# Turning the gated features by VectorE blocks and SBUF transfers, and adding the last products by copy and accumulating transfer, in a fused encoder layer

## The chip, the cores and the metric

One Trainium2 chip, one of its cores. The metric is the device time of the whole layer in microseconds (us). The kernel before takes 1175.23 us, the median of three runs.

## What is computed

A hybrid encoder layer over 256 rows of 2048 features: a mixing part (neighbourhood attention beside a gated recurrence), a SwiGLU feed-forward part of width 5632, and a gated embedding at the end, each with RMS norms. The change lies in the feed-forward part:

```python
fn = rms_norm(h, g_ffn_pre[i])
ff = (jax.nn.silu(fn @ w_ffn_gate[i]) * (fn @ w_ffn_up[i])) @ w_ffn_down[i]
h = h + rms_norm(ff, g_ffn_post[i])
```

## The kernel before

Every product is in float32 precision from three products of rounded parts: a weight tile `w` (two blocks of 128 input features, 512 columns, 512 KB) is loaded by SP into a raw tile, ScalarE (ACT) rounds it to `wh` (L464), VectorE (DVE) takes `wl = w - wh` (L489), and TensorE (PE) multiplies the split activations `hi`, `lo` with `wh`, `wl`, `wh` (L528 to L530). Six slots hold `wh`/`wl` and four the raw tiles; tiles that other stages lend (`lent_w`, `lent_r`, `lent_t`) add to them.

The feed-forward part runs in three parts of 4, 4 and 3 gate groups. A gate group makes 512 gate and 512 up columns from eight pairs of input blocks. Five pairs are plain (kind `p`: two weight tiles, 24 matmuls); three are of kind `s`, Strassen's seven products: 21 matmuls, for which DVE forms two more weight tiles out of the two loaded (`lent_t`, L509 and L513). The seven products end in four banks `p1 p5 p6 p7` and four banks `c11 c21 c12 c22`. When a group's last `s` pair is done, `Seven.early` takes the p banks into the tiles `e` (printed `mid`) and `u_hi`, `u_lo`; when its last pair is done, `Gated.late` adds the four c banks to them on DVE (L1589). ACT takes silu of `e` (L1616), DVE multiplies by `u` (L1596).

The gated features then have the 256 rows on partitions, and w_ffn_down needs the features there. `transposed` (L315) turns them on PE, four 128x128 transposes for each two blocks, into a bank; `split` (L295 on ACT, L297 on DVE) makes `hi` and `lo` of it (`mid0h`, `mid0l`, and so on). After the gate groups of a part, two down groups (one in the last part, with two plain segments behind it) multiply with w_ffn_down. `DOWN` says in which order and kind they take the pairs of blocks; `mid_sums` makes the sums that `s` pairs need of the activations. `Down.late` adds the down products to `mg` in SBUF.

All instructions are written in the order that a planner (`Plan`) chooses at build time from a table of costs: each engine then runs its list in order, and an instruction whose inputs are late holds all that stand behind it on its engine. Weight loads stand in SP's list; each waits for a raw tile that DVE has released.

Of the kernel before, what the change touches and what calls it, by code (L numbers as in the profile page):

```python
# [16 lines left out]
P = 128  # L17
# [26 lines left out]
for _n, _w in (  # L44
# [10 lines left out]
T_BUFS = 2  # L55
W_MORE = 1
# [11 lines left out]
LATE_SUMS = 0.0  # L68
FIRST = "ppppspsp"
KINDS = "ppspspsp"  # L70
HALF = max(2 * KINDS.count("s") * 4 * P, 2 * 1024)
# [156 lines left out]

def dma(kb, take=None):
    return ("dma", kb / 340.0, None, take, None)  # L230
# [3 lines left out]
def layer(ctx: ExitStack, tc: tile.TileContext, a: dict, out: bass.AP):  # L234
# [6 lines left out]
        wr=R_BUFS, w=W_BUFS, ts=0, acc=ACC_BUFS, sm=SM_BUFS, ev=1, mid=2, bt=2, uv=1  # L241
# [36 lines left out]
    ones = const.tile([P, P], F32, name="ones")  # L278
    nc.gpsimd.memset(ones, 1.0)
# [63 lines left out]
    class Act:  # L343
# [10 lines left out]
        def blocks(self, hi, lo, base, n, first=0):  # L354
            for i in range(n):
                self.at[base + i] = (hi[:, first + i, :], lo[:, first + i, :])
# [18 lines left out]
    class Group:  # L375


        def __init__(self, w, n0, lhs, ks, kinds, post, after=None):
            self.after = after
            self.lhs, self.post, self.banks, self.i0 = lhs, post, {}, len(tiles)  # L380
            self.early = Event()
            self.units = list(zip(ks, kinds))
            self.early = Event()
            for (k, _), kind in self.units:
                i = len(tiles)
                tiles.extend((w[c], k, n0[c]) for c in range(2))
                by_dma.update({"d": (i, i + 1), "e": (i + 1,), "c": (i,)}.get(kind, ()))
                if kind == "s":
# [82 lines left out]
    def add_raw(i):  # L471
        yield added(512)
        nc.gpsimd.dma_start(los[i], raws[i], accum_op=ALU.add)
        landed = Event()
        landed.t = plan.now + LANDED
        yield landed
        done(ev_lo[i, 2])
        used(i)
# [40 lines left out]
    def products(i, kx, lhs, accs, ts, start, stop, at=0.0):  # L519
        for j in range(2):  # L520
            here = ev_lo[i, j + 1] if (i, j + 1) in ev_lo else ev_lo[i, 2]
            plan.main(6 * MM * len(ts) / NT, here, lhs.ev[kx + j], at=at)
            wh, wl = his[i], los[i]
            hi, lo = lhs.at[kx + j]
            for t in ts:
                sl = slice(t * P, (t + 1) * P)
                st, sp = start and j == 0, stop and j == 1
                nc.tensor.matmul(accs[t], hi[:, sl], wh[:, j, :], start=st, stop=False)  # L528
                nc.tensor.matmul(accs[t], hi[:, sl], wl[:, j, :], start=False, stop=False)  # L529
                nc.tensor.matmul(accs[t], lo[:, sl], wh[:, j, :], start=False, stop=sp)  # L530
            at_pe[0] = max(at_pe[0], i)
            if j:
                free_w(i)
            plan.run()
# [11 lines left out]
    def seven(i, kx, g, start, stop):  # L546

        for name, v, j, which in FORMS:
            n = i + v
            if isinstance(which, tuple):  # L550
                kk, t = which
                (hi, lo), ev = g.lhs.at[kx + kk], g.lhs.ev[kx + kk]
                hi, lo = hi[:, t * P : (t + 1) * P], lo[:, t * P : (t + 1) * P]
# [14 lines left out]
    def run_group(g, flip):  # L568
# [5 lines left out]
        strassens = [n for n, (_, kind) in enumerate(g.units) if kind == "s"]  # L574
        for n, ((_, kx), kind) in enumerate(g.units):
            if kind == "s":
                seven(i, kx, g, n == strassens[0], n == strassens[-1])
                i += 4
                if n == strassens[-1]:
                    plan.add(g.post.early(g), plan.clk["pe"] + plan.SEM)  # L580
                    plan.run()
                continue
# [7 lines left out]
        plan.add(g.post.late(g), plan.clk["pe"] + plan.SEM)  # L590
# [139 lines left out]
    def open_p1():  # L730
        t1["hs"], t1["rec_hi"] = big(0, "hs", F32), big(1, "rec_hi")
        p1 = p1_ctx.enter_context(tc.tile_pool(name="p1", bufs=1))
        t1["pool"] = p1
        xp = p1.tile([P, HB, S + 4], F32, name="xp")
# [23 lines left out]
        nc.gpsimd.memset(ssr, 0.0)  # L758
# [3 lines left out]
    ssr = const.tile([P, S], F32, name="ssr")  # L762
    ssa = const.tile([P, S], F32, name="ssa")
# [151 lines left out]
    def group_rstd(ss, name):  # L915
# [3 lines left out]
        nc.tensor.matmul(pb[:, 0, :], ones, ss, start=True, stop=True)  # L919
        rb = const.tile([P, S], F32, name=f"rb_{name}")  # L920
# [15 lines left out]
    def gate_pair(b0, b, e, ev):  # L936
# [9 lines left out]
        yield from add_squares(ssr, sq, False)  # L946
        done(ev)

    def yg_post(hf):
        def post(ch):  # L950
# [13 lines left out]
            rb = yield from group_rstd(ssr, "rec")  # L964
# [132 lines left out]
    def attend(g):  # L1097
        ph, pl, vh, vl, sq, attnT = (t1[n] for n in ("ph", "pl", "vh", "vl", "sqa", "attnT"))
        yield ev_v[g]
        for b in range(0, HB, 2):  # L1100
# [23 lines left out]
            yield from add_squares(ssa, sq, h == 0)  # L1124
# [3 lines left out]
        ra = yield from group_rstd(ssa, "attn")  # L1128
# [249 lines left out]
    def mid_sums(mid, ks):  # L1378
        rs = t2["pool"]
        a_ = rs.tile([P, 2, 2, 4, P], F32R, tag="ple0", name="sums_a")  # L1380
        b_ = rs.tile([P, 2, 4, P], F32R, tag="pT", name="sums_b")
        at_ = [(a_[:, n, 0, :, :], a_[:, n, 1, :, :]) for n in range(2)]
        at_.append((b_[:, 0, :, :], b_[:, 1, :, :]))
        for k, (hi, lo) in zip(ks, at_):
            mid.sums[k] = hi, lo
            yield mid.ev[k]
            yield mid.ev[k + 1]
            yield dve(2 * S, take="uv")
            v = at.tile([P, 2, NT, P], F32, tag="at0_hi", name="v")
            nc.vector.tensor_tensor(  # L1390
                out=v.rearrange("p k t m -> p k (t m)"), in0=f32(mid.pair_of(k, 0)),
                in1=f32(mid.pair_of(k, 1)), op=ALU.add,
            )
            yield from act_sums(mid, k, v)

# [18 lines left out]
    def transpose_h(b, hi, lo, nxt, gname):  # L1414
# [20 lines left out]
        yield from act_sums(nxt, b, v)  # L1435
# [20 lines left out]
    def act_sums(x, b, v):  # L1456

        s = at.tile([P, 4, P], F32, tag="at0_lo", name="s")
        for n, i0, i1, op in (
            (0, v[:, 0, 1, :], v[:, 1, 1, :], ALU.add),  # L1460
            (1, s[:, 0, :], v[:, 0, 0, :], ALU.subtract),
            (2, v[:, 0, 0, :], v[:, 0, 1, :], ALU.subtract),
            (3, v[:, 1, 0, :], s[:, 1, :], ALU.subtract),
        ):
            yield dve(P)
            nc.vector.tensor_tensor(out=s[:, n, :], in0=i0, in1=i1, op=op)
# [63 lines left out]
    class Mid(Act):  # L1530
        def __init__(self, name):
            super().__init__()
            self.name, self.halves = name, {}
# [8 lines left out]
        def pair_of(self, k, which):  # L1542
            i, j = divmod(k, 8)
            return self.halves[i][which][:, j : j + 2, :]
# [31 lines left out]
    class Gated(Seven):  # L1576


        def __init__(self, mid, kk0):
            self.mid, self.kk0 = mid, kk0  # L1580

        def late(self, g):
# [3 lines left out]
            gated = [Event() for _ in range(NT)]  # L1586
            for t, c, n, x in self.parts():
                yield dve(N)
                nc.vector.tensor_tensor(out=x, in0=bk[n], in1=x, op=ALU.add)  # L1589
                g.give(n)  # L1590
                if not c:
                    plan.add(self.silu(t, gated[t]), plan.now)
            for t in range(NT):
                yield gated[t]
# [4 lines left out]
                )  # L1599
            plan.free["uv"].append(plan.now)  # L1600
            for b in range(0, 4, 2):
                tr = yield from transposed(e, b, g.ring["c11"])
                if b == 2:
                    plan.free["mid"].append(plan.now)
                kk = self.kk0 + b
                i, j = divmod(kk, 8)
                hi, lo = self.mid.tiles(i)
                yield from split(
                    hi[:, j : j + 2, :], lo[:, j : j + 2, :], tr, 2 * S, give=g.ring["c11"]
                )  # L1610
                self.mid.pair(kk)

        def silu(self, t, ev):
# [7 lines left out]
    class Down(Seven):  # L1621
# [5 lines left out]
        def late(self, g):  # L1627
            yield g.early
            mg, c0 = t2["mg"], self.c0
            for t, c, n, x in self.parts():  # L1630
# [7 lines left out]
                g.give(n)  # L1638
            plan.free["mid"].append(plan.now)
# [4 lines left out]

    def after_ffn():
        return next_norm(ffn, hP, rstd_p, ev_rp, ("ple", "g_ple_post"))

    hF.ev_sums = {k: Event() for k, kind in zip(ORDER, KINDS) if kind == "s"}

    parts = ((0, 4), (4, 8), (8, 11))  # L1650
    for part, (f0, f1) in enumerate(parts):
        mid = Mid(f"mid{part}")
        for f in range(f0, f1):
            Group(("w_ffn_gate", "w_ffn_up"), (f * N, f * N), hF,
                  [(k, k) for k in ORDER], KINDS if f else FIRST, Gated(mid, (f - f0) * 4))
        last_lent[0] = len(tiles)
        last = part == len(parts) - 1
        units = [[(u[0], int(u[1:])) for u in us.split()] for us in DOWN[f1 - f0]]
        summed = []
        for us in units[:1] if last else units:  # L1660
            summed += [k for kind, k in us if kind == "s" and k not in summed]
        mid.ev_sums = {k: Event() for k in summed}
        for n in range(1 if last else 2):
# [3 lines left out]
                  after=(lambda mid=mid, ks=summed: plan.add(  # L1667
                      mid_sums(mid, ks), plan.clk["pe"], LATE_SUMS)) if n == 0 else None)
# [189 lines left out]
```

## Time and profile before

| | before |
|---|---|
| median of three runs | 1175.23 us (1174.59 to 1175.87) |
| profiled execution: own time, span | 1173.45 us, 1171.7 us |
| granted clock | 0.997 |
| busy PE, DVE, ACT | 1150.5, 961.3, 701.9 us |
| HBM read | 232.6 MB, 203 GB/s over the span |

The profile is of one execution. Busy times of an engine are sums over its instructions where they don't overlap; a matmul's recorded length is longer than the step to the next one, so PE looks busy also where small gaps lie, and the steps between starts are the better measure. The feed-forward part runs from about 405 to 1045 us of the span.

### The profile page before, as it was taken

The numbers are of one execution on the slowest core, as the hardware profiler recorded it, in microseconds if no ns is written. First come the engines' busy times: TensorE is split into PE (matmuls) and PEld (weight loads), VectorE is DVE, ScalarE is ACT, GpSimd is POOL, SyncE is SP. The second block draws the span as 40 slices with busy tenths as digits, with TensorE's granted clock in tenths as the row PEclk, the third lists the DMA queues.
The fourth block names the chain that finished last, engine by engine and source line by source line (L and its number), as shares of the span: only waits on it lengthen the run. The fifth ranks groups of instructions, "written<-read, shape, count | busy, mean of one in ns | idle before, by whom it ended". The sixth has DMA issues, their size and how long they took to land.

```text
span 1171.7 us, 14652 instructions
## 1 busy us (share of the span) xinstructions
PE 1150.5 (98%) x5259; PEld 951.6 (81%) x5259; DVE 961.3 (82%) x1267; ACT 701.9 (60%) x952; POOL 1.6 (0%) x13
## 2 busy tenths in 40 slices
PE   7999999999999999999999999999999999999996
PEld 5788888888888888888888888888888888887885
DVE  5677868778549898898989899889999989888663
ACT  6787777766548655563665556554536446466752
POOL 0000000000000000000000000000000000000000
PEclk9999999999999999999999999999999999999998
DMA  8855555545864865664775475575567456775751
GB/s 307 288 173 180 176 187 197 164 158 168 313 229 141 302 191 180 224 214 146 226 256 192 159 245 182 173 238 160 191 207 242 153 180 229 261 246 190 241 171 72
DMA packets 70344, 238.80 MB, mean 204 GB/s; under 512 B 7552, under 2 KB 13824, under 8 KB 68864
## 3 DMA queue, kind: packets, MB, share of 16 engines
q1 hardware_dynamic: 70128, 237.79, 60.9%
q8 instruction: 41, 0.67, 0.2%
q14 instruction: 31, 0.25, 0.1%
q10 hardware_dynamic: 144, 0.08, 0.0%
HBM read 232.60 MB, written 5.24 MB: 203 GB/s over the span
## 4 chain that ended last, share of the span: by engine, by line
PE 82%; DVE 6%; DMA 6%; ACT 3%; issue 1%; SPq 1%; DVEq 0%; ACTq 0%
PE c L528 12%; PE c L530 12%; PE c L529 12%; PE acc L530 9%; PE acc L528 9%; PE acc L529 9%; PE p L538 3%; PE p L539 3%; PE p L537 3%; DVE wl L489 3%; PE c L537 2%; PE c L538 2%; PE c L539 2%; PE tr L315 2%; DMA wr<-in_w_ffn_down 1%; DMA xs<-in_xT 1%
## 5 line engine op out<-in xcount | busy, mean ns | idle before, releaser
L489 DVE TENSOR_TENSOR wl<-wr,wh 128x1024 fp32r<-128x1024 f32 (+1 forms) x311 | 358.4, 1167 | 76.0 <-ACT wh L464 75.1
L464 ACT CAST wh<-wr 128x1024 fp32r<-128x1024 f32 (+1 forms) x311 | 307.8, 1008 | 138.8 <-PE acc L530 46.7
L528 PE MATMUL c<-wh,hT_mix_hi 128*128 128x512 f32 x400 | 157.4, 394 | 0.0
L530 PE MATMUL c<-wh,hT_mix_lo 128*128 128x512 f32 x400 | 155.9, 390 | 0.0
L529 PE MATMUL c<-wl,hT_mix_hi 128*128 128x512 f32 x400 | 155.8, 389 | 0.0
L464 ACT CAST wh<-lent_t 128x1024 fp32r<-128x1024 f32 x75 | 78.7, 1052 | 113.0 <-DVE lent_t L513 105.7
L528 PE MATMUL acc<-wh,hT_hi 128*128 128x512 f32 x320 | 127.9, 400 | 6.6 <-ACT wh L464 6.6
L529 PE MATMUL acc<-wl,hT_hi 128*128 128x512 f32 x320 | 125.6, 392 | 1.8 <-DVE wl L489 1.8
L530 PE MATMUL acc<-wh,hT_lo 128*128 128x512 f32 x320 | 125.5, 392 | 0.0
L489 DVE TENSOR_TENSOR wl<-lent_t,wh 128x1024 fp32r<-128x1024 f32 x75 | 89.6, 1218 | 1.3 <-ACT wh L464 1.1
L530 PEld LDWEIGHTS c<-wh,hT_mix_lo 128*128 128x128 f32 x400 | 75.1, 188 | 16.0 <-DVE hT_mix_lo L303 0.2
L529 PEld LDWEIGHTS c<-wl,hT_mix_hi 128*128 128x128 f32 x400 | 75.2, 188 | 15.0
L528 PEld LDWEIGHTS c<-wh,hT_mix_hi 128*128 128x128 f32 x400 | 75.1, 188 | 15.0
L489 DVE TENSOR_TENSOR wl<-lent_r,wh 128x1024 fp32r<-128x1024 f32 (+1 forms) x70 | 76.3, 1102 | 4.7 <-ACT wh L464 4.5
L464 ACT CAST wh<-lent_r 128x1024 fp32r<-128x1024 f32 (+1 forms) x70 | 65.1, 957 | 23.9 <-PE c L530 15.2
L528 PEld LDWEIGHTS acc<-wh,hT_hi 128*128 128x128 f32 x320 | 60.6, 189 | 18.1 <-ACT wh L464 6.6
L529 PEld LDWEIGHTS acc<-wl,hT_hi 128*128 128x128 f32 x320 | 60.4, 189 | 14.9 <-DVE wl L489 3.4
L530 PEld LDWEIGHTS acc<-wh,hT_lo 128*128 128x128 f32 x320 | 60.3, 189 | 12.7
L530 PE MATMUL acc<-wh,hT_ffn_lo 128*128 128x512 f32 x112 | 43.7, 390 | 0.9 <-DVE hT_ffn_lo L303 0.9
L528 PE MATMUL acc<-wh,hT_ffn_hi 128*128 128x512 f32 x112 | 44.0, 393 | 0.0
L529 PE MATMUL acc<-wl,hT_ffn_hi 128*128 128x512 f32 x112 | 43.6, 389 | 0.0
L1616 ACT ACTIVATE mid<-mid,rstd_f 128x512 f32<-128x512 f32 x22 | 14.7, 716 | 28.8 <-DVE mid L1589 28.8
(439 smaller groups left out, 2334.8 us busy)
## 6 DMA issues: line engine op xcount, KB each, us to landing
wr<-in_w_in SPq DMA_DIRECT2D x79, 512.0 KB, 4.4
wr<-in_w_ffn_down SPq DMA_DIRECT2D x68, 512.0 KB, 4.3
wr<-in_w_ffn_gate SPq DMA_DIRECT2D x60, 512.0 KB, 4.2
wr<-in_w_ffn_up SPq DMA_DIRECT2D x60, 512.0 KB, 4.7
wr<-in_w_out SPq DMA_DIRECT2D x32, 512.0 KB, 4.7
wr<-in_w_ple_gate SPq DMA_DIRECT2D x32, 512.0 KB, 4.3
lent_r<-in_w_ffn_gate SPq DMA_DIRECT2D x28, 512.0 KB, 4.2
lent_r<-in_w_ffn_up SPq DMA_DIRECT2D x28, 512.0 KB, 4.5
```

Of the source, the lines that this page charges most:

```text
L315: nc.tensor.transpose(tr[:, b, t * P : (t + 1) * P], src, ident)
L464: nc.scalar.copy(his[i][:, j, :], raws[i][:, j, :])
L489: nc.vector.tensor_tensor(out=los[i][:, j, :], in0=raws[i][:, j, :], in1=f32(his[i][:, j, :]), op=ALU.subtract,)
L528: nc.tensor.matmul(accs[t], hi[:, sl], wh[:, j, :], start=st, stop=False)
L529: nc.tensor.matmul(accs[t], hi[:, sl], wl[:, j, :], start=False, stop=False)
L530: nc.tensor.matmul(accs[t], lo[:, sl], wh[:, j, :], start=False, stop=sp)
L537: nc.tensor.matmul(o, lh, wh, start=start, stop=False)
L538: nc.tensor.matmul(o, lh, wl, start=False, stop=False)
L539: nc.tensor.matmul(o, ll, wh, start=False, stop=stop)
L1616: nc.scalar.activation(self.e[:, t, :], self.e[:, t, :], AF.Silu, scale=rstd_f[:, t : t + 1])
```

## The change

1. The gated features are no longer turned by PE. After the multiplication DVE transposes each 128x512 tile in 32x32 blocks (L1603), and SP then issues 16 SBUF-to-SBUF transfers of 32 KB, which put the 32-row strips at their partitions in a tile `turned` (`turn`, L1633). The features stand in another order by this, so the rows of w_ffn_down are put in that order on the host. `split` reads `turned` in SBUF in place of a bank.
2. The last adds of a gate group: ACT copies a c bank to SBUF (`cp`, L1647, three tiles), and a transfer issued by GpSimd (POOL) accumulates it into `e` or `u` (`add_to`, L484). The very last gate group keeps DVE's adds (`hurry`).
3. The last adds of a down group: in the first part ACT copies the bank to `mg` and a transfer accumulates `e` or `u` into it; in the other parts DVE adds the bank to `e` or `u`, and a transfer accumulates that into `mg`. Where there were two DVE adds there is one, and where there was one there is none.
4. The sums for `s` pairs of the activations are made from `turned` within the gate groups; `mid_sums` is gone. There is room for two of them, not three: in the second down group of the first two parts the pair `s8` becomes `p8`, and the orders in `DOWN` change.
5. Some small tiles (`ones`, `ssr`, `ssa`, `rb`) move to a pool that ends before the feed-forward part.

PE has 88 transposes fewer and 6 matmuls more; the lists of all engines are as before up to the end of the first gate group (save for setup fills on POOL) and nearly so after the feed-forward part.

```diff
+CP_BUFS = 3
+SHARED = 2.6
+TURN = 4.0
+TURN_LATE = -4.0
 DOWN = {
-    4: ("p2 p6 p10 p8 s0 p12 s4 p14", "p2 p6 s0 p10 s4 p12 s8 p14"),
-    3: ("p2 p6 p10 s0 p4 p8", ""),
+    4: ("p2 p6 s0 p8 p10 s4 p12 p14", "p2 p6 s0 p10 s4 p12 p8 p14"),
+    3: ("p2 p4 s0 p6 p8 p10", ""),
 }
...
+def turn():
+    return ("dma", TURN, None, None, None)
...
+    def add_to(out, src, kb):
+        yield added(kb)
+        plan.clk["dma"] = max(plan.clk["dma"], plan.now - ADDED) + SHARED * kb / 512
+        nc.gpsimd.dma_start(out, src, accum_op=ALU.add)
         landed = Event()
         landed.t = plan.now + LANDED
         yield landed
...
     class Gated(Seven):
         def late(self, g):
...
             for t, c, n, x in self.parts():
-                yield dve(N)
-                nc.vector.tensor_tensor(out=x, in0=bk[n], in1=x, op=ALU.add)
-                g.give(n)
-                if not c:
-                    plan.add(self.silu(t, gated[t]), plan.now)
+                plan.add(self.sum_up(g, n, t, c, x, gated[t][c]), plan.now)
             for t in range(NT):
...
                 nc.vector.scalar_tensor_tensor(
                     out=e[:, t, :], in0=u[t], scalar=rstd_f[:, t : t + 1], in1=e[:, t, :],
                     op0=ALU.mult, op1=ALU.mult,
                 )
+                yield dve(N)
+                nc.vector.transpose(e[:, t, :], e[:, t, :])
...
+            plan.add(self.turn(e, raw, there), plan.now, TURN_LATE)
+            yield there
...
+            for t in range(NT):
+                yield from split(hi[:, t], lo[:, t], raw[:, t], N)
             for b in range(0, 4, 2):
-                tr = yield from transposed(e, b, g.ring["c11"])
...
+        def turn(self, e, raw, there):
+            yield turn()
+            for c in range(4):
+                for a_ in range(4):
+                    nc.sync.dma_start(
+                        raw[c * 32 : (c + 1) * 32, a_, :, :],
+                        e[a_ * 32 : (a_ + 1) * 32, :, c * P : (c + 1) * P],
+                    )
+            done(there)
+
+        def sum_up(self, g, n, t, c, x, ev):
+            if self.hurry:
+                yield dve(N)
+                nc.vector.tensor_tensor(out=x, in0=g.banks[n], in1=x, op=ALU.add)
+                g.give(n)
+            else:
+                yield act(N, take="cp")
+                tmp = t2["pool"].tile([P, N], F32, tag="cp", name="cp", bufs=CP_BUFS)
+                nc.scalar.copy(tmp, g.banks[n])
+                g.give(n)
+                yield from add_to(x, tmp, 256)
+                plan.free["cp"].append(plan.now)
...
     class Down(Seven):
         def late(self, g):
...
                 if self.part:
                     yield dve(N)
-                    nc.vector.tensor_tensor(out=to, in0=x, in1=to, op=ALU.add)
-                    x = to
-                yield dve(N)
-                nc.vector.tensor_tensor(out=to, in0=g.banks[n], in1=x, op=ALU.add)
+                    nc.vector.tensor_tensor(out=x, in0=g.banks[n], in1=x, op=ALU.add)
+                else:
+                    yield act(N)
+                    nc.scalar.copy(to, g.banks[n])
                 g.give(n)
+                landed.append(Event())
+                plan.add(self.to_mg(to, x, landed[-1]), plan.now)
...
+        if n == "w_ffn_down":
+            w = w.reshape(k // N, 4, 4, 32, m).transpose(0, 2, 1, 3, 4).reshape(k, m)
```

DVE's list at the end of the second gate group, before. The first row is the last of the four early adds; `mid<-c`, `u<-c` are the adds of the c banks, `lent_t` the sums for an `s` pair, `lent_w` and `wl` the weights' low parts.

```order
L1565 TENSOR_TENSOR u_lo<-p_3724,mid 128x512
L489 TENSOR_TENSOR wl<-wr,wh 128x1024
L509 TENSOR_TENSOR lent_t<-lent_r 128x512
L1589 TENSOR_TENSOR mid<-c_3611,mid 128x512
L1589 TENSOR_TENSOR mid<-c_3612,mid 128x512
L1589 TENSOR_TENSOR u_hi<-c_3631,u_hi 128x512
L489 TENSOR_TENSOR wl<-wr,wh 128x1024
L1589 TENSOR_TENSOR u_lo<-c_3632,u_lo 128x512
L1596 SCALAR_TENSOR_TENSOR mid<-u_hi,rstd_f,mid 128x512
L1596 SCALAR_TENSOR_TENSOR mid<-u_lo,rstd_f,mid 128x512
L489 TENSOR_TENSOR lent_w<-lent_r,lent_w 128x1024
L513 TENSOR_TENSOR lent_t<-lent_r 128x512
```

The same place of DVE's list now, from the second weight tile after the early adds to the two block transposes.

```order
L503 TENSOR_TENSOR lent_w<-lent_r,lent_w 128x1024
L523 TENSOR_TENSOR lent_t<-lent_r,lent_t 128x512
L503 TENSOR_TENSOR wl<-lent_r,wh 128x512
L527 TENSOR_TENSOR lent_t<-lent_r,lent_t 128x512
L503 TENSOR_TENSOR wl<-lent_t,wh 128x1024
L1598 SCALAR_TENSOR_TENSOR mid<-u_hi,rstd_f,mid 128x512
L1603 STREAM_TRANSPOSE mid<-mid 128x512
L503 TENSOR_TENSOR wl<-lent_t,wh 128x1024
L1598 SCALAR_TENSOR_TENSOR mid<-u_lo,rstd_f,mid 128x512
L1603 STREAM_TRANSPOSE mid<-mid 128x512
L503 TENSOR_TENSOR wl<-wr,wh 128x1024
```

The four bank adds are gone, and the gating multiplications stand behind the weights of the next `s` pair, where they stood ahead of all of them. Behind the rows shown stand seven more of weights and sums, then the first split from `turned`.

ACT's list at the same place, before: `mid<-p` is the copy of the first p bank, then casts of weights, silu, and the first split of a turned bank.

```order
L1553 COPY mid<-p_3704 128x512
L464 CAST lent_w<-lent_r 128x1024
L464 CAST wh<-lent_r 128x512
L1616 ACTIVATE mid<-mid,rstd_f 128x512 x2
L295 CAST mid0h_3662<-tr 128x512
```

And now: `cp<-c` are the new copies of the c banks.

```order
L1558 COPY mid<-p_3706 128x512
L474 CAST wh<-wr 128x1024 x2
L474 CAST lent_w<-lent_r 128x1024
L474 CAST wh<-lent_r 128x512
L1647 COPY cp<-c_3611 128x512
L1647 COPY cp<-c_3612 128x512
L1647 COPY cp<-c_3638 128x512
L474 CAST wh<-lent_t 128x1024
L1656 ACTIVATE mid<-mid,rstd_f 128x512
L1647 COPY cp<-c_3639 128x512
L1656 ACTIVATE mid<-mid,rstd_f 128x512
```

Three bank copies stand ahead of the first silu, and the fourth behind it, so the fourth can't start before the first silu, which reads what the first transfer lands. On SP the 16 transfers of this group stand in one run, between two weight loads.

More of the change, by code (lines that the diff above doesn't have):

```diff
@@ L68 @@
 LATE_SUMS = 0.0
+LATE_EVAC = 0.0
+EARLY_EVAC = 0.0
 FIRST = "ppppspsp"
 KINDS = "ppspspsp"
-HALF = max(2 * KINDS.count("s") * 4 * P, 2 * 1024)
+HALF = max(2 * sum(k in "st" for k in KINDS) * 4 * P, 2 * 1024)
 ORDER = (0, 2, 4, 6, 8, 10, 12, 14)
@@ L1376, in ple_back @@
         nc.sync.dma_start(t2["ple", 0], t2["kept", "ple"])
[L1378 to L1394, printed above, removed]
     def give_back():
@@ L1613, in silu @@
-        def silu(self, t, ev):
+            n = self.kk0 // 4
+            if not n:
+                self.mid.open()
+            raw = self.mid.raw
+            there = Event()
+            plan.add(self.turn(e, raw, there), plan.now, TURN_LATE)
+            yield there
+            plan.free["mid"].append(plan.now)
+            i, j = divmod(self.kk0, 8)
+            hi, lo = (x[:, j : j + 4, :].rearrange("p b (t a i) -> p t a b i", t=NT, a=4)
+                      for x in self.mid.tiles(i))
```

145 lines of the change are left out of this document (81 added, 64 removed).

## The prediction

> **What bounds the kernel now.** I read the page first, then the busy times of the feed-forward stretch, then PE, DVE, ACT and SP in order of time around one group's end.
>
> ```profile
> PE 1150.5 (98%) x5259; PEld 951.6 (81%) x5259; DVE 961.3 (82%) x1267; ACT 701.9 (60%) x952; POOL 1.6 (0%) x13
> 405.00:1045.00 640.00, 640.00 (x2867) 530.03 (x2867) 584.88 (x718) 348.18 (x399) 0.00 (x0) 1.00 0.62 204
> L315 PE MATMUL tr<-ident,mid x88: 270/272/273, 412.6 to 1007.6; 128*128 128x128 f32 x88
> ```
>
> The second row is the stretch that the change touches: PE has 2867 instructions in 640 us at full granted clock, DVE is busy 91% of it, ACT 54%, the DMA engines 62%. The third is the group that goes. Busy PE alone proves little, so I count steps between starts.
>
> ```profile
> 404.84 0.39 PE L530 MATMUL c<-wh,hT_mix_lo 128*128 128x512 f32 x1
> ...
> 412.09 0.39 PE L529 MATMUL c<-lent_w,hT_mix_hi 128*128 128x512 f32 x1
> 412.32 0.40 PE L530 MATMUL c<-lent_w,hT_mix_lo 128*128 128x512 f32 x1
> 412.55 0.60 PE L315 MATMUL tr<-ident,mid 128*128 128x128 f32 x4
> 412.91 0.48 PE L528 MATMUL c<-lent_w,hT_mix_hi 128*128 128x512 f32 x1
> 413.23 0.39 PE L529 MATMUL c<-lent_w,hT_mix_hi 128*128 128x512 f32 x1
> ```
>
> From 404.84 to 412.09 lie 32 matmuls: 0.2266 us each. From 412.32 to 413.23 lie two matmuls and four transposes, 0.91 us, so four transposes take 0.91 - 0.45 = 0.457 us. 88 of them take 22 x 0.457 = 10.05 us; the other 2779 take 2779 x 0.2266 = 629.7. Together 639.8 of 640: PE never waits in this stretch, and what PE is spared comes off the end as long as PE still never waits.
>
> How near is the next engine? At the end of the second gate group:
>
> ```profile
> 443.65 0.69 DVE L1556 TENSOR_TENSOR mid<-p,mid 128x512 f32<-128x512 f32 x1 [1.30 <-ACT mid L1553]
> ...
> 446.44 1.21 DVE L489 TENSOR_TENSOR wl<-wr,wh 128x1024 fp32r<-128x1024 f32 x1
> 447.57 0.68 DVE L509 TENSOR_TENSOR lent_t<-lent_r 128x512 f32<-128x512 f32 x1
> 448.17 1.28 DVE L1589 TENSOR_TENSOR mid<-c,mid 128x512 f32<-128x512 f32 x2
> ...
> 451.70 0.74 DVE L1596 SCALAR_TENSOR_TENSOR mid<-u_hi,rstd_f,mid 128x512 f32<-128x512 f32 x1
> 452.36 0.74 DVE L1596 SCALAR_TENSOR_TENSOR mid<-u_lo,rstd_f,mid 128x512 f32<-128x512 f32 x1
> ...
> 461.88 1.22 DVE L489 TENSOR_TENSOR wl<-lent_t,wh 128x1024 fp32r<-128x1024 f32 x1
> 463.02 1.22 DVE L489 TENSOR_TENSOR wl<-wr,wh 128x1024 fp32r<-128x1024 f32 x1
> ...
> 537.51 0.28 DVE L1466 TENSOR_TENSOR s<-v 128x128 f32<-128x128 f32 x1
> ```
>
> ```profile
> 442.73 0.39 PE L528 MATMUL c<-wh,hT_mix_hi 128*128 128x512 f32 x1
> ...
> 463.62 0.39 PE L538 MATMUL p<-wl,sums_f 128*128 128x512 f32 x1
> 464.98 0.39 PE L529 MATMUL c<-wl,hT_mix_hi 128*128 128x512 f32 x1
> ```
>
> The `wl` of the last sum tile is done at 461.88 + 1.22 = 463.10, and PE reads it at 463.62: 0.5 us to spare. The next is done at 464.24 for 464.98. So DVE is close behind PE once a group, though PE sets the end. Its steps are 1.13 us for 1024 columns (446.44 to 447.57), 0.60 for 512 (to 448.17), 0.66 for a gating product (451.70 to 452.36); a sum of 128 columns takes 0.28. The group's last pair starts on PE at 442.73 and ends 24 matmuls, 5.44 us, later, at 448.17.
>
> **What PE gains.** 88 transposes go: -10.05 us. Two pairs turn from `s` (21 matmuls) to `p` (24): +6 x 0.2266 = +1.36. Sum -8.69 us. The profiled execution takes 1173.45 us, so 1164.8; the median of the runs lies 1.78 above that execution, so 1166.5 in its terms.
>
> **What the others gain or pay.** DVE loses 40 bank adds in ten gate groups, 20 in the down groups and the seven adds of `mid_sums`, and gains 22 block transposes. The trace shows no block transpose. Its bounds are the 512-column step, 0.60, and the 1024-column step, 1.13; I take 0.60, since it streams 512 columns. Net (22 - 67) x 0.60 = -27 us, besides the sums of two `s` pairs. ACT gains 48 copies:
>
> ```profile
> 442.09 1.05 ACT L464 CAST wh<-wr 128x1024 fp32r<-128x1024 f32 x1 [0.20 <-DMA wr<-in_w_ffn_up]
> 443.04 0.58 ACT L1553 COPY mid<-p 128x512 f32<-128x512 f32 x1
> 443.52 1.05 ACT L464 CAST lent_w<-lent_r 128x1024 fp32r<-128x1024 f32 x1
> 445.01 0.62 ACT L464 CAST wh<-lent_r 128x512 fp32r<-128x512 f32 x1 [0.44 <-PE c L530]
> 448.88 1.34 ACT L1616 ACTIVATE mid<-mid,rstd_f 128x512 f32<-128x512 f32 x2 [3.25 <-DVE mid L1589]
> ```
>
> A copy is 0.48 (443.04 to 443.52), a cast 0.95, a silu 0.67: 48 x 0.48 = 23 us in an engine with 290 us free. The DMA engines get 60 accumulating transfers of 256 KB and 176 turning ones of 32 KB, 21.5 MB beside the 130 MB (204 GB/s x 640 us) that make 62%: 72% at the same rate, about 90% if each of these bytes costs three times as much. No engine is full. What can cost time is the new chain of waits.
>
> **The chain, walked through once.** The prices of transfers:
>
> ```profile
> 460.76 0.33 SPq L439 DMA_DIRECT2D lent_r<-in_w_ffn_gate  x1
> 461.19 0.38 SPq L439 DMA_DIRECT2D lent_r<-in_w_ffn_up  x1
> L1735 SPq DMA_DIRECT2D out<-h x8: 332/332/344, 1155.2 to 1168.4; - x8
> DMA to landing us min/median/max: 1.8/2.2/2.5
> L439 SPq DMA_DIRECT2D wr<-in_w_ffn_gate x60: 327/328/518, 335.2 to 974.2; - x60
> DMA to landing us min/median/max: 2.7/4.4/9.2
> ```
>
> SP issues one each 0.43 us, so the 16 turning transfers hold SP 6.9 us; the weight load behind them waits as long. Their landing is bounded by the quiet stores (1.8) and the weight loads (9.2); I take the stores' 2.2, small transfers on a queue that holds only themselves. An accumulating transfer from POOL is not in the trace at all. Its landing is bounded the same way; I take 4.4, the median of the weight loads: half their bytes, amid their traffic, but the target is read too. The Trainium skill, "DMA: Bandwidth & Descriptors", Anatomy of one DMA, gives 2.0 us plus bytes over 436 GB/s for a POOL-issued one, an estimate of 2.6 us here; no run here shows one yet, and by it the sum stays and the first rival below would hardly happen.
>
> Now the second gate group, on the clock of the rows above, with PE's needs 0.91 us earlier from the two transpose sets that go. DVE's early adds start at 443.65, take 2.79 (to 446.44) and let one weight tile in: 447.57. The list then has three tiles, a half and four sums (4.0 + 2.4): the last sum is ready at 454.0. ACT, behind casts, copies the first bank by 447.45 and the third by 448.9 (its products end with the pair at 448.17). The first landing is at 447.45 + 4.4 = 451.85, silu to 452.75, and only then the fourth bank's copy, to 453.25: in ACT's list it stands behind silu. PE next takes these banks for the first `s` pair, 10.9 us after 448.17, so they come free in time. DVE: the first sum's `wl` to 455.1, first gating and transpose to 456.35, second sum's `wl` to 457.5, which PE needs at 462.7: 5.2 us to spare where there were 0.5. The fourth landing is at 453.25 + 4.4 = 457.65: DVE waits 0.15, second gating and transpose to 458.9. Three more tiles, a half and four sums (6.4) take DVE to 465.3. Meanwhile SP issues from 458.9 to 465.8, the last lands at 468.0, ACT casts it by 468.6: DVE stands 3.3 us before its split, and the weights queued behind it wait too. Then split, `wl`, split, a small sum, `wl` (0.60, 1.13, 0.60, 0.28, 1.13): the last sum tile of the second `s` pair is done at 472.3. PE starts the plain pair before it one matmul ahead of 464.98 less 0.91, at 463.84, and needs that tile 5.44 + 16 x 0.2266 later, at 472.9. **0.6 us to spare.** So by these prices PE still never waits, but DVE's slack is used up: each us on top of 0.6 is a us per group. With an accumulating landing 1 us later the chain is 2 us later, since the fourth copy waits for the first landing.
>
> How many groups? In the last gate group of a part the turned blocks are needed late (six pairs, four `p` and two `s`, 4 x 5.44 + 2 x 4.76 = 31 us into the down group; 21 us in the last part, where DVE adds directly), and DVE has less to do. That leaves eight tight groups (3 + 3 + 2). A block transpose at 1.13 instead of 0.60 would cost 2 x 0.53 - 0.6 = 0.5 us in each, 4 us in all. For the forecast I add 0.8 us of small waits (0.1 each).
>
> **The rivals.** *Accumulating transfers land late.* At 6.0 us the chain is 3.2 us later, 2.6 over, in eight groups 21 us: 1166.5 + 21 = 1187.5 us. It decides from about 5.2 us on, where 1.1 us per group eat the 8.69. For it: each shares the DMA engines with weight loads, whose landing reached 9.2. Against: the 4.4 median with twice the bytes.
>
> *The turning transfers are slow.* Sixteen of 32 KB, each with a fixed price:
>
> ```profile
> L808 SPq DMA_DIRECT2D av<-in_w_rg_a x8: 378/450/471, 51.7 to 183.5; - x8
> DMA to landing us min/median/max: 2.2/4.1/5.1
> ```
>
> These loads, 128 KB each in a row, land after 4.1. With that for 2.2 each group is 1.9 later, 1.3 over: 10 us, so 1166.5 + 10 = 1176.5, no gain. The Trainium skill says on the same page, under Rules for kernel authors, that transfers under 64 KB are mostly overhead and should be made one; these rows bear it out in part, since 128 KB land hardly sooner than 512 KB.
>
> *The transposes were hidden anyway*: excluded by the count to 639.8 of 640.
>
> **How the numbers follow.** Forecast, PE without waits: 0.65. Late accumulating transfers: 0.24. Slow turning: 0.11. The likeliest gives 1166.5 + 0.8 = 1167.3 us; its own range is 1164.5 (about an execution as quick as the profiled one) to 1172. A measurement of this kernel can tell about 0.2%, 2.35 us, from no change. The forecast lies wholly below that, slow turning lies around it (0.08 within, 0.03 slower), late landings above: faster 0.65, same 0.08, slower 0.27. The range to 1181 takes in slow turning and the milder third of late landings.
>
> **What would show it.** In the changed kernel's profile the stretch should have some 2785 PE instructions in about 631 us and no PE wait. Late landings would show as DVE waiting ahead of the gating product (L1598) and ACT ahead of silu (L1656), both released by DMA; slow turning as ACT and DVE waiting ahead of the splits (L303, L305); either with PE waiting for `wl`. Landings near 3 us would leave about 2 us more slack than I walked. The forecast is wrong if PE's step in the stretch is above 0.2266 on the mean by over 0.5%.

## The result, and the profile after

| | before | after |
|---|---|---|
| median (4 runs each) | 1174.91 us | 1237.09 us (1235.63 to 1239.76) |
| ratio, 95% interval | | 1.0531 (1.0511 to 1.0551) |
| profiled execution: own time, span | 1173.45, 1171.7 us | 1239.76, 1238.0 us |

The change makes the kernel 5.3% slower; 1167.3 us was forecast. The page's busy line after:

```profile
PE 1168.1 (94%) x5177; PEld 953.7 (77%) x5177; DVE 926.9 (75%) x1200; ACT 722.8 (58%) x994; POOL 54.5 (4%) x73
```

The stretch from 405 to 1045 us and a short window around one wait (length, then PE, PEld, DVE, ACT, POOL busy with counts, granted clock, DMA share, GB/s):

```profile
405.00:1045.00 640.00, 598.02 (x2548) 484.99 (x2547) 502.16 (x595) 337.40 (x401) 49.36 (x56) 0.98 0.70 211
434.00:446.00 12.00, 6.53 (x20) 4.89 (x19) 7.12 (x13) 4.00 (x6) 0.00 (x0) 0.72 0.53 187
```

PE got 2548 instructions into the 640 us that held 2867 before. DVE and ACT are less busy, not more: everybody waits. The longest waits on the new transfers, by the engine that waits and what ended them (total us, times, longest us):

```profile
ACT mid1h L303 <- DMA turned<-mid: 31.7, 4, 9.1
ACT mid0h L303 <- DMA turned<-mid: 29.5, 4, 8.0
ACT mid2h L303 <- DMA turned<-mid: 21.0, 3, 9.0
DVE mid1l L305 <- ACT mid1h L303: 23.6, 4, 6.7
ACT mid L1656 <- DMA mid<-cp: 21.5, 12, 5.3
DVE mid L1598 <- DMA u_hi<-cp: 14.7, 5, 5.4
```

Both signs that the prediction named for its rivals are there: splits that wait for the turned strips (31.7 + 29.5 + 21.0 = 82 us on ACT, in all eleven groups), and silu and gating that wait for accumulating transfers. The prices, from the DMA issues (count, KB each, median us to landing):

```profile
turned<-mid SPq DMA_DIRECT2D x176, 32.0 KB, 1.9
mid<-cp POOLq DMA_DIRECT2D x20, 256.0 KB, 6.1
u_hi<-cp POOLq DMA_DIRECT2D x10, 256.0 KB, 8.1
u_lo<-cp POOLq DMA_DIRECT2D x10, 256.0 KB, 6.6
```

SP's timeline at the first group (start, length, engine, line, transfer, count):

```profile
425.40 11.23 SPq L1633 DMA_DIRECT2D turned<-mid  x16
436.74 0.52 SPq L449 DMA_DIRECT2D lent_r<-in_w_ffn_gate  x1
```

The strips land as fast as hoped (1.9 us), but 16 issues hold SP 11.2 us (0.70 each), not 6.9; in the other groups it is 10.2 to 11.2. The accumulating transfers land after 6.1 to 8.1 us, not 4.4. The second group, the one that was walked, in the timelines of ACT, SP and DVE, one after the other:

```profile
456.43 1.55 ACT L1647 COPY cp<-c 128x512 f32<-128x512 f32 x3
463.88 0.72 ACT L1656 ACTIVATE mid<-mid,rstd_f 128x512 f32<-128x512 f32 x1 [3.21 <-DMA mid<-cp]
464.51 0.57 ACT L1647 COPY cp<-c 128x512 f32<-128x512 f32 x1
485.91 0.62 ACT L303 CAST mid0h<-turned 128x512 fp32r<-128x512 f32 x1 [7.09 <-DMA turned<-mid]
...
474.26 10.18 SPq L1633 DMA_DIRECT2D turned<-mid  x16
...
469.06 0.75 DVE L1598 SCALAR_TENSOR_TENSOR mid<-u_hi,rstd_f,mid 128x512 f32<-128x512 f32 x1 [5.45 <-DMA u_hi<-cp]
472.74 0.75 DVE L1598 SCALAR_TENSOR_TENSOR mid<-u_lo,rstd_f,mid 128x512 f32<-128x512 f32 x1 [1.07 <-DMA u_lo<-cp]
473.52 0.71 DVE L1603 STREAM_TRANSPOSE mid<-mid 128x512 f32<-128x512 f32 x1
474.16 1.18 DVE L503 TENSOR_TENSOR wl<-wr,wh 128x1024 fp32r<-128x1024 f32 x1
486.56 0.69 DVE L305 TENSOR_TENSOR mid0l<-turned,mid0h 128x512 fp32r<-128x512 f32 x1 [5.94 <-ACT mid0h L303]
```

The chain has the shape that was walked: three copies, silu, the fourth copy behind it, gating, transposes, the turn, the split. DVE stands idle in it for 5.45 + 1.07 + 5.94 = 12.5 us, with the weights of the next pair queued behind each wait. What PE pays for that in the first group:

```profile
434.83 0.39 PE L541 MATMUL c<-wh,hT_mix_hi 128*128 128x512 f32 x1
440.69 0.79 PE L542 MATMUL c<-wl,hT_mix_hi 128*128 128x512 f32 x1 [5.47 <-DVE wl L503]
441.28 0.63 PE L543 MATMUL c<-wh,hT_mix_lo 128*128 128x512 f32 x1
...
445.12 0.47 PE L543 MATMUL c<-wh,hT_mix_lo 128*128 128x512 f32 x1
445.43 0.39 PE L550 MATMUL p<-wh,hT_mix_hi 128*128 128x512 f32 x1
```

A wait, and then nine steps of 0.427 us (441.28 to 445.12) instead of 0.2267: the window row above has the granted clock at 0.72. Over all PE rows from 405 to 1110 us, the steps exceed 0.2267 us per matmul by 74.6 us in sum; 63 slow steps make 12.6 us of it. (The same sum is 2.3 us in the kernel without waits below.)

### The profile page after: what moved, and what is told of

It is laid out like the page before. It is cut to its first block, busy times and chain, and to the rows that moved or that the text cites. A ratio compares the mean times of both kernels' runs of the same rounds, so it can differ in the third digit from the quotient of the medians.

```text
span 1238.0 us, 14919 instructions
## 1 busy us (share of the span) xinstructions
PE 1168.1 (94%) x5177; PEld 953.7 (77%) x5177; DVE 926.9 (75%) x1200; ACT 722.8 (58%) x994; POOL 54.5 (4%) x73
## 4 chain that ended last, share of the span: by engine, by line
PE 51%; issue 16%; DVE 12%; DMA 9%; SPq 6%; ACT 3%; POOL 2%; ACTq 0%; DVEq 0%; POOLq 0%
PE acc L543 10%; PE acc L542 10%; PE acc L541 10%; SPq L1633 6%; DVE wl L503 5%; PE c L541 5%; PE c L543 5%; PE c L542 5%; DMA u_lo<-cp 3%; ACT wh L474 1%; DMA lent_r<-in_w_ffn_up 1%; PE p L551 1%; DMA turned<-mid 1%; PE p L552 1%; PE p L550 1%
## 5 line engine op out<-in xcount | busy, mean ns | idle before, releaser
L503 DVE TENSOR_TENSOR wl<-wr,wh 128x1024 fp32r<-128x1024 f32 (+1 forms) x322 | 372.2, 1170 | 89.5 <-ACT wh L474 88.8
L474 ACT CAST wh<-wr 128x1024 fp32r<-128x1024 f32 (+1 forms) x322 | 319.6, 1010 | 154.7 <-PE acc L543 54.0
L542 PE MATMUL c<-wl,hT_mix_hi 128*128 128x512 f32 x400 | 158.8, 397 | 16.5 <-DVE wl L503 16.5
L474 ACT CAST wh<-lent_t 128x1024 fp32r<-128x1024 f32 x72 | 75.1, 1051 | 114.8 <-DVE lent_t L527 99.5
L503 DVE TENSOR_TENSOR wl<-lent_t,wh 128x1024 fp32r<-128x1024 f32 x72 | 87.0, 1219 | 17.3 <-ACT wh L474 16.9
L503 DVE TENSOR_TENSOR wl<-lent_r,wh 128x1024 fp32r<-128x1024 f32 (+1 forms) x58 | 63.0, 1097 | 1.5 <-ACT wh L474 1.5
L474 ACT CAST wh<-lent_r 128x1024 fp32r<-128x1024 f32 (+1 forms) x58 | 53.9, 951 | 15.3 <-PE c L543 11.6
L484 POOL DMA_DIRECT2D mid<-cp x20 | 17.7, 985 | 761.7 <-DMA wr<-in_w_ffn_up 487.8
```

Source lines behind the costliest of these rows:

```text
L474: nc.scalar.copy(his[i][:, j, :], raws[i][:, j, :])
L484: nc.gpsimd.dma_start(out, src, accum_op=ALU.add)
L503: nc.vector.tensor_tensor(out=los[i][:, j, :], in0=raws[i][:, j, :], in1=f32(his[i][:, j, :]), op=ALU.subtract,)
L542: nc.tensor.matmul(accs[t], hi[t], wl[:, j, :], start=False, stop=False)
```

## The experiments

Theory S: the 16 issues hold SP too long, so the turned strips come late. Theory L: the accumulating transfers land late. A kernel without any wait should come to PE's count, 1166.5 us. One run each unless an interval is given; before took 1174.0 to 1174.5 us beside the single runs, and 1175.26 us in the median beside the five rounds.

**Both cuts, one at a time and together.** Four transfers in place of 16 (in `turn`):

```diff
-            for c in range(4):
-                for a_ in range(4):
-                    nc.sync.dma_start(
-                        raw[c * 32 : (c + 1) * 32, a_, :, :],
-                        e[a_ * 32 : (a_ + 1) * 32, :, c * P : (c + 1) * P],
-                    )
+            for a_ in range(4):
+                nc.sync.dma_start(raw[:, a_, :, :], e[:, :, a_ * P : (a_ + 1) * P])
```

> The 16 turning transfers of a group become 4 of 128 partitions each, with the same bytes; they leave the features in other places than the product needs, so the output is another, and the order of all other instructions is unchanged. Theory S (the 16 issues hold SP's list 11.2 us a group, which starves the weight loads and delays the splits): SP is held about 2 us a group, the waits ahead of L303 and L305 shrink to under a third, and the time is 1180 to 1195 us. Theory L (the accumulating transfers land after 6 to 8 us and hold ACT and DVE): DVE's waits ahead of L1598 and ACT's ahead of L1656 stay, and the time is still above 1220 us.

A quarter of each accumulating transfer (in `sum_up`):

```diff
-                yield from add_to(x, tmp, 256)
+                yield from add_to(x[:, 0:P], tmp[:, 0:P], 256)
```

> The accumulating transfers of the gate groups move 128 of the 512 columns (64 KB instead of 256 KB), so three quarters of those adds are left out; the order is unchanged, the 16 turning transfers stay. Theory L: landings of about 3 us, the waits ahead of L1598 and L1656 go, and the time falls to 1200 us or less. Theory S: the time stays at 1217 to 1230 us.

> Both cuts of the two kernels before: 4 turning transfers instead of 16, and accumulating transfers of a quarter of the columns. If S and L together are the whole loss, PE hardly waits between 405 and 1045 us and the time is 1166 to 1172 us. If it stays above 1180 us, something else (the copies on ACT, the new order of the lists, POOL) costs the rest.

Measured: 1176.79 us with four issues, 1217.59 with quarter adds, 1165.82 with both. SP's row in the kernel with four issues:

```profile
424.93 2.68 SPq L1632 DMA_DIRECT2D turned<-mid  x4
```

Theory S had that kernel at 1180 to 1195 us; it came out a little below. Two of the waits that are left there:

```profile
ACT mid L1656 <- DMA mid<-cp: 22.2, 12, 5.0
DVE mid L1598 <- DMA u_hi<-cp: 14.3, 5, 5.5
```

The stretch of the kernel with both cuts:

```profile
405.00:1045.00 640.00, 640.00 (x2825) 530.13 (x2824) 558.73 (x661) 379.18 (x451) 52.90 (x60) 1.00 0.74 229
```

Together the two cuts take away the whole loss, and PE never waits in the stretch: 2825 instructions in 640 us are 0.2265 each. In this order of the lists the larger part is S: 60.3 us go with the 12 issues, 19.5 with three quarters of the added bytes. The two overlap: 79.8 in sum, 71.3 with both. An issue takes SP 0.67 us (2.68 / 4) for 128 partitions as for 32, so the price is per transfer and not per byte. L alone, with four issues, costs 11.0 us (1176.79 - 1165.82): its waits of 22.2 and 14.3 us are as long as before the cut (21.5 and 14.7), and most of them no longer reach PE.

**Is it the starved weight stream, or the late strips?** While SP issues strips it issues no weight loads (rows 425.40 and 436.74). POOL is nearly idle, so there the strips can be issued without holding them:

```diff
-                    nc.sync.dma_start(
+                    nc.gpsimd.dma_start(
                         raw[c * 32 : (c + 1) * 32, a_, :, :],
```

> The 16 turning transfers of a group are issued by POOL instead of SP; nothing else moves in the lists. POOL's issues took 0.87 us each, so the last turned strip comes some 3 us later than from SP, but SP issues weight loads in the meantime. Theory S1 (the loss is the starved weight stream): 1185 to 1205 us. Theory S2 (the loss is that ACT and DVE stand before their splits, with the weights' casts and differences queued behind them, while the weights themselves are there): 1240 to 1270 us, and ACT's wait ahead of L303 grows from 82 us to over 100 us.

1250.85 us. SP issues a weight load during the turn (first row of the timelines below), and still ACT waits for the strips:

```profile
430.89 0.33 SPq L449 DMA_DIRECT2D wr<-in_w_ffn_gate  x1
436.73 0.62 ACT L303 CAST mid0h<-turned 128x512 fp32r<-128x512 f32 x1 [6.96 <-DMA turned<-mid]
```

Its waits for them are a little longer than before:

```profile
ACT mid1h L303 <- DMA turned<-mid: 35.3, 4, 11.6
ACT mid0h L303 <- DMA turned<-mid: 33.2, 4, 8.9
ACT mid2h L303 <- DMA turned<-mid: 23.7, 3, 9.0
```

So S1 falls. The strips are as late from POOL as from SP: in the first group the split starts 12.2 us after the first issue (424.51 to 436.73), where it was 12.8 (425.40 to 438.16). The growth of the waits was smaller than expected (92 us, not over 100). What costs is the wait in the lists of ACT and DVE.

**Undoing either half, or both.** DVE adds the c banks again:

```diff
-                  [(k, k) for k in ORDER], KINDS if f else FIRST, Gated(mid, (f - f0) * 4, last and f == f1 - 1))
+                  [(k, k) for k in ORDER], KINDS if f else FIRST, Gated(mid, (f - f0) * 4, True))
```

> The second part of the change is undone for the gate groups: DVE adds the c banks as before, with no copies by ACT and no accumulating transfers there; the turning by DVE blocks and SP transfers stays. DVE has 40 adds of 0.60 us, 24 us, more again. Theory S with L as the smaller part: near the kernel with quarter adds, 1210 to 1225 us. If DVE's 24 us count in full: 1230 us or more. If late landings are the larger part after all: under 1200 us.

PE turns again (`late` calls `transposed` as before, `w_ffn_down` keeps its rows; the transfers stay for the adds):

```diff
-                yield dve(N)
-                nc.vector.transpose(e[:, t, :], e[:, t, :])
...
+                tr = yield from transposed(e, b, g.ring["c11"])
```

> The turning part is undone: PE turns the features again by 88 transposes (10.05 us more on PE), and w_ffn_down keeps its order of rows; the copies and accumulating transfers of the last adds stay. Without any waits PE's count gives 1166.5 + 10.05 = 1176.5 us. Theory S: 1177 to 1182 us, since only the turning costs. Theory L: 1195 us or more, since the late landings hold ACT and DVE with either way of turning.

Both of these edits in one kernel:

> Both the turning and the gate groups' adds are undone (PE turns, DVE adds the c banks); the accumulating transfers of the down groups and the new orders of pairs stay. PE has its 10.05 us of transposes again, so without waits 1174.2 us (the kernel before) plus 1.4 us for two pairs made plain is 1175.6. Near that, 1174 to 1178 us, the rest of the change is free and the whole loss lies in turning and adds; above 1185 us it costs by itself.

Measured: 1236.90 us with DVE's adds, 1204.07 with PE's turn, and 1178.10 (ratio 1.0026, 1.0014 to 1.0038) with both. DVE's adds and the accumulating transfers cost the same as long as the turn is late (it was 1230 us or more that was expected if DVE's 24 us count in full). The kernel with PE's turn came out where theory L had it, not at the 1177 to 1182 us of theory S: beside the kernel with both undone the accumulating transfers cost 26 us there (1204.07 - 1178.10), far more than the 11.0 with four issues. PE's own transposes then stand in PE's list and wait for the gating, and the gating waits for `u_lo`:

```profile
PE tr L323 <- DVE mid L1598: 8.5, 7, 2.1
DVE mid L1598 <- DMA u_lo<-cp: 26.1, 10, 4.8
```

So the 11 to 20 us of L hold only in the lists of the changed kernel. With both undone the rest of the change costs 0.26%, about 3 us, of which six matmuls more are 1.4.

**The planner's prices.** The lists of ACT, DVE and SP are written by a planner, whose table in the change has the turn at 4.0 us of SP and a landing at 2.5. The trace has 10.2 to 11.2, and 6.1 to 8.1. Only these two numbers are changed, the landing's to a value still below the trace's medians:

```diff
-LANDED = 2.5
+LANDED = 5.0
-TURN = 4.0
+TURN = 11.2
```

> Only the planner's prices are changed, to what the trace of the changed kernel shows: the turning takes SP 11.2 us (4.0 in the change) and an accumulating transfer lands 5.0 us (2.5) after its issue. The work is the same, the lists are re-planned. Theory P (the loss comes of lists planned with wrong prices): 1175 to 1200 us. Theory R (the held queue and the late landings cost as much in any order): 1220 us or more.

1173.03 us, and once more in five rounds:

> The kernel with both corrected prices (turning 11.2, landing 5.0) once more, timed in five rounds beside the kernel before. PE's count says 1166.5 us without waits, the first run 1173.0 with 7 us of waits left: 1171.5 to 1174 us, between 0.3% faster and no change.

The median is 1176.01 us, above the 1171.5 to 1174 that were expected, and the ratio to before is 1.0005 (0.9993 to 1.0016): no change, with the same work and the same transfers that cost 5.3% in the other order. PE's gain is not there either: the waits that are left eat it (1176.01 - 1166.5 = 9.5 us). The second group in its timeline, first run:

```profile
466.70 0.71 DVE L1603 STREAM_TRANSPOSE mid<-mid 128x512 f32<-128x512 f32 x1
467.33 0.65 DVE L503 TENSOR_TENSOR wl<-wr,wh 128x512 fp32r<-128x512 f32 x1
...
478.86 1.21 DVE L503 TENSOR_TENSOR lent_w<-wr,lent_w 128x1024 fp32r<-128x1024 f32 x1
480.00 1.28 DVE L305 TENSOR_TENSOR mid0l<-turned,mid0h 128x512 fp32r<-128x512 f32 x2
467.44 10.20 SPq L1633 DMA_DIRECT2D turned<-mid  x16
479.06 1.14 ACT L303 CAST mid0h<-turned 128x512 fp32r<-128x512 f32 x2 [0.88 <-DMA turned<-mid]
```

SP is held as long as before (10.20 us) and the strips come as late; but DVE has 12.7 us of weights (467.33 to 480.00) between its last transpose and its split, where the changed kernel has 6.5 (474.16 to 480.62), and ACT's wait is 0.88 instead of 7.09. Each price alone, the turn's (`TURN = 11.2`, `LANDED = 2.5`) and the landing's (`TURN = 4.0`, `LANDED = 5.0`):

> Of the two corrected prices only the turning's: the planner counts 11.2 us of SP for it (4.0 in the change), the accumulating transfer's landing stays at 2.5. Theory P (the loss of 62.8 us comes of splits that stand too early in ACT's and DVE's lists): the waits ahead of L303 and L305 nearly go, and what the late landings cost by themselves is left, 11 us by the pair of kernels with 4 transfers: 1177 to 1187 us. If both prices are needed for it: over 1200 us.

> Of the two corrected prices only the landing's: 5.0 us (2.5 in the change); the turning stays at 4.0 us of SP. Theory P: the waits ahead of L1598 and L1656 nearly go, as with quarter adds, and the splits still stand too early: 1212 to 1230 us. If the landing's price alone repairs the lists: under 1195 us.

And the 16 transfers planned one by one:

```diff
-TURN = 4.0
+TURN = 0.7
...
             for c in range(4):
                 for a_ in range(4):
+                    if not first:
+                        yield turn()
+                    first = False
                     nc.sync.dma_start(
```

> The planner takes the 16 turning transfers one by one (0.7 us each), so weight loads may stand between them on SP, and the splits are planned by the true length of their issue. Theory S1: weight loads go on in between, 1185 to 1205 us. Theory S2: the last strip still comes 11 us or more after the first issue; where the planner puts the splits later in ACT's and DVE's lists by as much, they wait less, 1190 to 1215 us; where it does not, 1235 us or more.

1201.77 us with the turn's price, 1222.57 with the landing's: 35.3 and 14.5 off, 49.8 in sum, where both at once take 64.1. Theory P's 1177 to 1187 for the turn's price alone was too low; the run came out where both prices are needed. Its waits ahead of L303 for the strips are nearly gone, 20.2 us in sum, no more than the 22.4 of the first run with both prices. The waits for landings stay: 25.1 us on ACT and 16.4 on DVE, where the kernel with both prices has 12.4 and 3.8 in its first run, and 13.6 and 16.4 in its five-round profile. It is ACT's waits, ahead of silu most of all, that set this run apart:

```profile
ACT mid L1656 <- DMA mid<-cp: 19.6, 10, 5.0
```

So 11 us is not the price of late landings in every order. The one-by-one planning gave 1199.92; its 16 issues still stood in one run of 10.9 us, so it is the turn's price in another form and says nothing on loads in between.

A landing price of 7.0 beside the turn's 11.2 was one step too far:

```diff
-LANDED = 5.0
+LANDED = 7.0
```

> Both prices, the landing at 7.0 us instead of 5.0 (the trace has medians of 6.8 to 9.2). If the remaining 7 us over the kernel without waits are still late landings: 1167 to 1171 us. If they are the turned strips, which still come later than planned: 1172 to 1175 us, as with 5.0.

1207.98 us. With this price, in two of the three parts, the planner puts the sums that an `s` pair needs (L1464) behind the next group's turn, so they are made from that group's features, and DVE waits for it with everything behind:

```profile
525.48 0.29 DVE L1464 TENSOR_TENSOR s<-turned 128x128 f32<-128x128 f32 x1 [10.69 <-DMA turned<-mid]
```

This time says nothing on the question that was asked.

**Fewer issues by way of DRAM.** Two writes into a DRAM tile and four reads take the place of the 16 transfers:

```diff
+            by = kept.tile([P, 4, NT, P], F32, name="by")
+            for t in range(NT):
+                yield turn()
+                nc.sync.dma_start(by[:, :, t, :], e[:, t, :].rearrange("p (c n) -> p c n", c=4))
...
+            by = by.rearrange("(a i) c t n -> c i a (t n)", i=32)
+            for c in range(4):
+                yield turn()
+                nc.sync.dma_start(
+                    raw[c * 32 : (c + 1) * 32].rearrange("i a t n -> i a (t n)"), by[c]
+                )
```

The prices are `TURN = 0.7` for each of the six and `LANDED = 7.0`; `BACK`, the time between the last write's and the first read's issue, is 0.5.

> The features are turned by way of a DRAM tile: 2 writes and 4 reads (6 issues) take the place of the 16 SBUF-to-SBUF transfers, planned at 0.7 us each; the landing is priced at 7.0 us. Fewer issues hold SP about 4 us a group, at the price of one more landing of some 2 us. If SP's hold and the landings are all that is left: 1165 to 1170 us, PE without waits. If the reads of DRAM land as late as weight loads (4 us and more) and the splits wait for them: 1172 to 1185 us.

> The kernel that turns by way of DRAM with the landing priced at 7.0, timed in five rounds: 1169.5 to 1172 us, 0.2 to 0.4% faster than before. If the first run was a lucky one: within 0.1% of before.

```diff
-BACK = 0.5
+BACK = 2.5
-LANDED = 7.0
+LANDED = 6.0
```

> The same way through DRAM with the prices nearer to the trace of its first run: 2.5 us instead of 0.5 between the writes' and the reads' issue (the writes landed after 4.5 us), the landing of accumulating transfers at 6.0 (4.9 to 6.8). If the waits left are those of splits that still stand too early: 1167 to 1170 us. If they lie at the ends of the parts, where the down group needs the last features whatever the order: 1170 to 1172 us, as before this edit.

1170.67 us in the first run, between the two ranges that were expected; in five rounds 0.9949 (0.9933 to 0.9966), and with the later prices 0.9950 (0.9935 to 0.9964): both beat the kernel before by half a per cent, and the last edit of prices is worth nothing that these runs can tell. SP's timeline in the last of them:

```profile
421.07 4.41 SPq L1634 DMA_DIRECT2D by<-mid  x2
425.58 0.56 SPq L450 DMA_DIRECT2D lent_r<-in_w_ffn_gate  x1
429.50 3.09 SPq L1641 DMA_DIRECT2D turned<-by  x4
```

Its stretch:

```profile
405.00:1045.00 640.00, 638.27 (x2811) 526.63 (x2810) 555.09 (x656) 376.02 (x446) 52.80 (x60) 1.00 0.85 250
```

The SP rows span 4.41 and 3.09 us, with weight loads between the two halves; the 4.41 is mostly the wait for the second tile, whose transpose DVE ends at 424.92. The strips themselves land later than from SBUF (5.2 us against 1.9). PE loses 1.7 us of the 640, with the DMA engines 85% busy. Fewer issues and later places in the lists came together here, and no run tells their shares apart.

## Why the prediction failed, step by step

**What bounds the kernel, and what PE gains: right.** The run with both cuts took 8.3 us less than before (1165.82 against 1174.16), where 8.69 was summed, and PE had no waits in the stretch. The block transpose's step, taken as 0.60, is 0.64 (473.52 to 474.16). The landing of the turning transfers, taken as 2.2, is 1.9.

**"SP issues one each 0.43 us": wrong.** The rows behind it were weight loads. The transfers between SBUF tiles took 0.64 to 0.70 each, 10.2 to 11.2 a group instead of 6.9. The rival "The turning transfers are slow" had the right waits (ahead of L303 and L305) for the wrong reason (landing), and it priced them at 10 us; with accumulating landings of 5.3 us and less they cost 52 (1217.59 - 1165.82).

**The accumulating landing, 4.4: too short.** It was 6.1 to 8.1 in the median. The rival asked for 6.0 and gave 21 us; what it costs depends on the lists around it, 11.0 us with four issues, 19.5 beside the 16 and 26 with PE's turn. The walk let only the first and the fourth landing bind; in the trace DVE's longest wait in that group, 5.45 us, is for the third (`u_hi`), the slowest of them at 8.1. The Trainium skill's figure that the prediction cited ("DMA: Bandwidth & Descriptors", Anatomy of one DMA: an estimate of 2.6 us) is contradicted: 256 KB took 6.1 to 8.1 us, and even 64 KB took 3.2 to 5.3 in the kernel with quarter adds. Why these transfers land so late was not tested.

**"0.6 us to spare", in "eight tight groups": wrong in both halves.** With the measured prices the walk is 1.7 later for the first landing, 2.2 for the fourth and 2.65 for the turn (474.16 to 485.91 against 9.1): 6.55 us, 5.95 over. In eight groups that is 48 us, in eleven 65; measured are 70.6 (1237.1 - 1166.5). The first group, never walked, loses 5.6 us at its first wait, and the last groups of the parts, written off as having time, wait as the others do (4 + 4 + 3 waits above). The walk also undersized the turn by itself: repriced it gives 2.05 us a group for that, while the kernel with quarter adds, whose landings are near the walked 4.4, loses more than that at one wait in each of the first two groups:

```profile
438.92 0.80 PE L542 MATMUL c<-wl,hT_mix_hi 128*128 128x512 f32 x1 [4.78 <-DVE wl L503]
...
483.17 0.79 PE L551 MATMUL p<-lent_w,sums_f 128*128 128x512 f32 x1 [5.28 <-DVE lent_w L503]
```

**"Each us on top is a us per group": too little.** Of the 74.6 us, 12.6 are no wait at all but PE's slower steps after waits.

**The step behind all of these** is that the lists were taken as given and walked with prices other than those by which they had been written. The kernel's table has the turn at 4.0 us and a landing at 2.5; the prediction's own prices were 6.9 and 4.4. A planner that believes the smaller numbers puts the split where the strips would then be ready, which is too early by the difference; this could be read beforehand, and it spoke against a chance of 0.65. That the same work costs nothing in another order is shown by the kernel with two numbers changed, which is level with before; PE's largest wait that is left in its feed-forward part, in its five-round profile, is 2.43 us. The kernel with both cuts shows the other side: the same order costs nothing when the transfers are quicker.

## What to carry to other kernels

Where a planner orders the lists, compare its price of each new operation with the nearest rows of the trace first: a price that is too low does not cost its error once, it puts a waiting instruction ahead of everything that could have run meanwhile. Count a queue's hold per transfer, from transfers of the same kind, and merge transfers before making them cheaper. A chain with 0.6 us to spare and three prices taken from other operations is a coin toss at best, and one group walked does not stand for its neighbours.

## What the runs showed of the hardware

After waits PE runs slowly for a time: nine such runs in the changed kernel, of 1 to 12 matmuls at 0.427 us, in sum 12.6 us, with the granted clock at 0.72 over 434 to 446 us. The Trainium skill, "TensorE: Matmul & The Clock Gate", Part 1: The HAM clock gate, gives 426.7 ns a step for a cold array and 215.7 for a warm one at 512 columns, and an idle window of about 3.4 us as the cause; the slow step agrees, the fast one is 0.2267 here. Here a slow run also followed a wait of 2.02 us (between 472.98 and 475.39), behind one of 1.32 us.

An SBUF-to-SBUF transfer from SP holds its queue 0.64 to 0.70 us whether it has 32 or 128 partitions, a weight load of 512 KB 0.43. An accumulating transfer of 64 KB lands after 3.2 to 5.3 us, one of 256 KB after 6.1 to 8.1 in the gate groups: four times the bytes, less than twice the time.
